# Gated DeltaNet block on one core: the first value convolution of the second half of heads, made behind the query convolutions instead of behind the decay exponentials

## The chip, the core and the metric

The kernel runs on one core of a Trainium2 chip. The core has five engines with queues of their own: TensorE (PE, matrix products; PEld is its weight load), VectorE (DVE), ScalarE (ACT), GpSimd (POOL) and SyncE (SP, which here issues the DMA transfers). Each engine works through its queue in order; semaphores make it wait for others. The metric is the device time of one execution in microseconds (us), as a median of runs.

## The reference

One transformer layer on x of 1024 tokens by 1024 features, in float32:

```python
h = _rmsnorm(x, norm_attn_g[l]) * (1.0 + sc1) + sh1
proj = h @ w_in[l]
q_a, k_a, v_a, q_d, k_d, v_d, z_d, b_d, a_d = jnp.split(proj, split_points, axis=-1)
y_attn = _dilated_attention(q_a, k_a, v_a, rel_bias)
y_delta = _gated_deltanet(q_d, k_d, v_d, z_d, b_d, a_d, conv_w[l], a_log[l], dt_bias[l], delta_norm_g[l])
x = x + g1 * (jnp.concatenate([y_attn, y_delta], axis=-1) @ w_out[l])
h = _rmsnorm(x, norm_ffn_g[l]) * (1.0 + sc2) + sh2
x = x + g2 * ((jax.nn.silu(h @ w_gate[l]) * (h @ w_up[l])) @ w_down[l])
```

The part that matters here is the DeltaNet: 8 heads of 64 features. Its q, k and v go through a causal convolution of width 4 along the tokens and a silu, q and k are normalised to length 1, and then a recurrence over chunks of 64 tokens follows:

```python
q, k, v = jnp.split(jax.nn.silu(_causal_conv(jnp.concatenate([q, k, v], axis=-1), conv_w)), 3, axis=-1)
a_mat = jnp.where(strict, jnp.einsum('nbhcd,nbhed->nbhce', k_beta, kc) * decay, 0.0)
rhs = jnp.concatenate([vc * bc[..., None], k_beta * jnp.exp(gcum)[..., None]], axis=-1)
sol = lax.linalg.triangular_solve(a_mat + jnp.eye(CHUNK), rhs, left_side=True, lower=True, unit_diagonal=True)
qk = jnp.where(causal, jnp.einsum('nbhcd,nbhed->nbhce', qc, kc) * decay, 0.0)
```

`decay` is the exponential of differences of a running sum, `u` and `w` are the two parts of `sol`, and a scan over the chunks carries a 64x64 state per head.

## The kernel before

The kernel computes the modulation, the normed input and the projections (each as three float32r products of high and low halves), the DeltaNet, the dilated attention, the output projection and the feed-forward part, in that order as a whole. The DeltaNet is made in two halves of 4 heads, `delta(0)` and `delta(1)`; a half has two pairs of heads, and a pair fills 128 partitions. Tiles of the second half bear the numbers 2 and 3: `vd2` and `vd3` are its convolved values, `kd2`, `qd2` and so on its keys and queries.

A half consists of these steps:

- Convolutions (`conv`, L549): a scaled copy on ACT (L551), three multiply-and-add steps on DVE (L553), a silu on ACT (L557). For the second half those of k and q are made early, in `delta_early` at the end of the first half, and go through DRAM (`cv_d`); `xp_k`, `xp_q`, `xp_v` are the loaded inputs.
- `delta_turn`: transposes on PE (`trq`, `trk`), squares on ACT (`sqq`, L744) and sums on DVE (`eq`, `rk`, L748), from which the norms come.
- `delta_rows` (L701): four loads of 512 KB that spread the decay's running sums over all partitions, into `dt1_0` to `dt1_3`, one per head. They have the tag `lu` with five buffers; `vd2` and `vd3` have the same tag.
- `delta_prep` (L756): `lr`, `rk` and `nbp` on ACT and DVE, a transpose of `nbp` on PE (`ps_bp`, L781), 32 exponentials of the decay on ACT (L771, 8 for each head), the products of k with k and of q with k on PE (`kk`, L800), their multiplication by the decay on DVE (L806), stores of its blocks to DRAM (`lt_d`, L813), exponentials `eb` on ACT (L839) and the product `qd` times `eb` on POOL (L840).
- `delta_v` (L845): for each pair the convolution of the values, transposes on PE (`trv`, L857), and the product with beta on DVE (`vb`, L860).
- `delta_inverse`: loads the blocks as `nt`, inverts them in a row of small DVE steps (L886, L890), goes through DRAM as `tn`, and completes the inverse on PE (`lv`, L918).
- `delta_scan`: the recurrence.

While these steps run, PE is given the matmuls of other projections as filling: `g_z` (the gate), `g_va` (the attention's values, L613) and, in between, `mods` (the modulation, L211). `turn(name)` puts an amount of this filling, by a table `FILL` of microseconds, ahead of a named step; the table has 12.8 for `trv2_0` and 10.24 for `trv3_0`. `until(...)` runs the filling until a projection is complete. What the program text says is then put in order, on each engine, by a list scheduler that goes by the order of the text, by its cost estimates and by explicit `issue_after` relations. So a part that is written elsewhere also changes the places of its neighbours.

Of the kernel before, what the change touches and what calls it, by code (L numbers as in the profile page):

```python
# [10 lines left out]
F32 = mybir.dt.float32  # L11
# [7 lines left out]
P = 128  # L19
# [63 lines left out]
def build(tc, I, out):  # L83
# [758 lines left out]
            )  # L842
        st.update(nbp=nbp, nbg=nbg, eq=eq, kt=kt, lts=lts, qks=qks, gs=gs)

    def delta_v(g, st, vps):  # L845
        st["vb"] = []
        for q in range(2):
            hp = 2 * g + q
            vd = pd.tile([P, T], F32, name=f"vd{hp}", tag="lu", bufs=5)
            conv(8 + hp, vps[q](), vd)  # L850
            vb = pd.tile([P, 8, P], F32, name=f"vb{hp}", tag="vb", bufs=2)
            bh = beta[:, st["gs"]].rearrange("p (n h) -> p n h", n=8)[:, :, 2 * q : 2 * q + 2]
            for hf in range(2):
                ps = sbank(f"trv{hp}_{hf}")
                with turn(f"trv{hp}_{hf}"):
                    for j in range(4):
                        nc.tensor.transpose(  # L857
                            ps[:, j * P : (j + 1) * P], vd[:, (4 * hf + j) * P : (4 * hf + j + 1) * P], ident
                        )
                nc.vector.tensor_tensor(  # L860
                    out=vb[:, 4 * hf : 4 * hf + 4].rearrange("p n (e d) -> p n e d", e=2),
                    in0=ps.rearrange("p (n e d) -> p n e d", n=4, e=2),
                    in1=bc(bh[:, 4 * hf : 4 * hf + 4], 64), op=ALU.mult,
                )
            st["vb"].append(vb)
# [324 lines left out]
    def fetch(i, name):  # L1190
        xp = pr.tile([P, T], F32, name=f"xp_{name}", tag="xp", bufs=2)
        nc.sync.dma_start(xp, _.pj[i])
        return xp

    def delta_early():

        for j in range(4):
            kind, q = ("k", j) if j < 2 else ("q", j - 2)
            t = pr.tile([P, T], F32, name=f"cv{j}", tag="dt", bufs=2)
            conv((4 if kind == "k" else 0) + 2 + q, fetch(j, f"{kind}{2 + q}"), t)  # L1200
            delta_turn(1, kind, q, t, norms=norms[1])
            nc.sync.dma_start(_.cv[j], t)

    marks = {}
    norms = [delta_norms(g) for g in range(2)]

    def delta(g):
        st = {}
        kt = []
        for j in range(4):  # L1210
            kind, q = ("k", j) if j < 2 else ("q", j - 2)
            hp = 2 * g + q
            t = pd.tile([P, T], F32, name=f"{kind}d{hp}", tag=f"{kind}d", bufs=2)
            (kd if kind == "k" else qd)[hp] = t
            if g == 0:
                conv((4 if kind == "k" else 0) + hp, xps[j], t)
                kt.append(delta_turn(g, kind, q, t, norms=norms[0], keep=kind == "k"))
                if j == 1:
                    nc.scalar.activation(norms[0]["lr"], norms[0]["rk"], AF.Ln, bias=eps1)
            else:  # L1220
                nc.sync.dma_start(t, _.cv[j])
                if kind == "k":
                    kt.append(delta_turn(g, kind, q, t, keep=True))
        delta_prep(g, st, norms[g], kt[0:2], delta_rows(g))
        if g == 1:
            until(lambda: "vd" in done)
        delta_v(g, st, [lambda q=q: vxp[q] if g == 0 else fetch(4 + q, f"v{2 + q}") for q in range(2)])
        delta_inverse(g, st)
        until(lambda: ("qd", "z1")[g] in done)
        delta_scan(g, st)  # L1230
        if g == 0:
            delta_early()

    delta(0)
    delta(1)
    until(lambda: EARLY - 1 in done)
    run(mods)

# [763 lines left out]
```

## Time and profile before

| what | value |
|---|---|
| median of 3 runs (lowest, highest) | 1402.27 us (1399.55, 1403.21) |
| the profiled execution | 1399.13 us |
| its span in the profile | 1397.3 us |
| PE busy | 1343.9 us, 96% of the span |
| DVE, ACT, POOL busy | 63%, 47%, 20% of the span |
| mean granted clock of PE | 0.991 |
| DMA, moved over the span | 245.68 MB |

The profile's page shows one execution. A row of a timeline has the start in us from the span's start, the length, the engine, the line of the kernel, the operation with output and inputs, the shape and the number of instructions that it stands for; in brackets stands how long the engine was idle ahead of it and what ended that. A row of waits has the waiting instruction, the one waited for, and then the time in total, how many times, and the longest. A row of a table of stretches has the stretch, its length, the busy time of each engine with the number of its instructions, then PE's granted clock (1.00 is full speed), the share in which the DMA engines were busy, and GB/s.

### The profile page before, as it was taken

What the parts mean: (1) busy time and instruction counts of PE and PEld (TensorE: products, weight loads), DVE (VectorE), ACT (ScalarE), POOL (GpSimd) and SP (SyncE); (2) the same over time, 40 slices, a digit from 0 to 9 for tenths busy, and PEclk for the clock granted to TensorE, in tenths of its full rate; (3) what the DMA queues carried; (4) which work ended last, traced back from release to release, by engine and by line L of the source; (5) the groups of instructions that cost most, each with busy time, mean ns of one, the idle gap of its engine ahead of it and who ended that gap; (6) DMA issues with size and microseconds to landing.
All of it is one profiled execution on the core that took longest, in us unless ns stands there. A gap on an engine that the chain in (4) does not pass through costs nothing.

```text
span 1397.3 us, 24428 instructions
## 1 busy us (share of the span) xinstructions
PE 1343.9 (96%) x8984; PEld 1109.9 (79%) x8984; DVE 878.8 (63%) x1677; ACT 661.4 (47%) x1287; POOL 283.6 (20%) x267
## 2 busy tenths in 40 slices
PE   8999999998999899999999999999999999999998
PEld 5778877888888777778877788888888888888876
DVE  3688484656836433676238977667575776474497
ACT  4498424356234254775157633333333333444455
POOL 2346412443213244443262000000000000000000
PEclk9999999999999999999999999999999999999999
DMA  8666575486352455541584355455453665766585
GB/s 310 230 190 168 160 212 168 131 259 184 106 152 69 124 141 177 152 110 58 187 269 151 113 159 181 158 163 173 133 200 108 213 210 191 255 222 192 195 262 197
DMA packets 169872, 245.68 MB, mean 176 GB/s; under 512 B 32566, under 2 KB 73831, under 8 KB 169752
## 3 DMA queue, kind: packets, MB, share of 16 engines
q1 hardware_dynamic: 169752, 244.12, 55.3%
q8 instruction: 71, 1.16, 0.3%
q14 instruction: 49, 0.40, 0.1%
HBM read 181.30 MB, written 67.48 MB: 178 GB/s over the span
## 4 chain that ended last, share of the span: by engine, by line
PE 53%; DVE 5%; DMA 3%; issue 2%; ACT 2%; POOL 1%; SPq 0%; DVEq 0%; ACTq 0%; POOLq 0%
PE wua L1596 9%; PE wga L1596 8%; PE X L1796 6%; PE wuc L1596 4%; PE wgc L1596 4%; PE wo L590 4%; PE g_a L590 3%; PE wgb L1596 2%; PE Z L1796 2%; PE Y L1796 2%; PE wub L1596 2%; PE y L1353 2%; PE tr L1332 2%; PE S L1308 1%; PE S L1309 1%
## 5 line engine op out<-in xcount | busy, mean ns | idle before, releaser
L1586 DVE TENSOR_TENSOR wl_db<-wr_db,wh_db 128x512 fp32r<-128x512 f32 x77 | 52.9, 690 | 66.4 <-ACT wh_db L1585 66.4
L1585 ACT CAST wh_db<-wr_db 128x512 fp32r<-128x512 f32 x77 | 47.4, 620 | 85.7 <-PE X L1796 39.4
L1312 DVE CUSTOM_DVE_ANT_0 X<-S,ng 128x512 f32<-128x512 f32 (+3 forms) x64 | 36.9, 587 | 57.2 <-PE S L1309 43.7
L1319 POOL TENSOR_SCALAR X<-X,sc 128x128 f32<-128x128 f32 (+7 forms) x64 | 48.7, 764 | 76.3 <-DVE sc L1318 72.3
L1796 PE MATMUL X<-wl_db,wh_da 128*128 128x512 f32 x160 | 62.4, 390 | 0.3 <-DVE wl_db L1586 0.3
L1796 PE MATMUL X<-wh_db,wl_da 128*128 128x512 f32 x160 | 62.3, 389 | 0.0
L1796 PE MATMUL X<-wh_db,wh_da 128*128 128x512 f32 x160 | 62.3, 389 | 0.0
L1317 ACT ACTIVATE X<-X,sc 128x128 f32<-128x128 f32 (+7 forms) x64 | 49.5, 775 | 24.3 <-DVE sc L1312 22.7
L1586 DVE TENSOR_TENSOR wl_da<-wr_da,wh_da 128x512 fp32r<-128x512 f32 x77 | 52.8, 685 | 3.7 <-ACT wh_da L1585 3.6
L1585 ACT CAST wh_da<-wr_da 128x512 fp32r<-128x512 f32 x77 | 47.5, 616 | 15.0 <-DMA wr_da<-ao_d 8.1
L590 PE MATMUL g_a<-hh,wh_a 128*128 128x512 f32 x128 | 52.7, 412 | 0.0
L590 PE MATMUL wo<-yl,wh_wo 128*128 128x512 f32 x128 | 50.6, 396 | 1.9 <-DVE yl L1416 1.9
L590 PE MATMUL g_a<-hh,wl_a 128*128 128x512 f32 x128 | 51.7, 404 | 0.0
L590 PE MATMUL wo<-yh,wh_wo 128*128 128x512 f32 x128 | 51.6, 406 | 0.0
L590 PE MATMUL g_a<-hl,wh_a 128*128 128x512 f32 x128 | 51.4, 401 | 0.0
L590 PE MATMUL wo<-yh,wl_wo 128*128 128x512 f32 x128 | 51.1, 399 | 0.0
L1332 PE MATMUL tr<-ident,X 128*128 128x128 f32 x288 | 45.8, 278 | 5.1 <-POOL X L1319 2.4
L1585 ACT CAST wh_wg_s<-wg_s 128x512 fp32r<-128x512 f32 x33 | 20.5, 623 | 57.6 <-PE wuc L1596 24.4
L1332 PEld LDWEIGHTS tr<-ident,X 128*128 128x128 f32 x288 | 32.8, 140 | 17.0 <-POOL X L1319 6.2
L231 POOL TENSOR_TENSOR wl_wo<-wr_wo,wh_wo 128x512 fp32r<-128x512 f32 x24 | 32.2, 1344 | 59.1 <-ACT wh_wo L230 54.9
L1585 ACT CAST wh_wu_s<-wu_s 128x512 fp32r<-128x512 f32 x33 | 20.4, 621 | 43.8 <-PE wga L1596 17.2
L1585 ACT CAST wh_wg<-wr_wg 128x512 fp32r<-128x512 f32 x31 | 19.2, 622 | 46.3 <-PE wua L1596 18.9
(553 smaller groups left out, 4370.0 us busy)
## 6 DMA issues: line engine op xcount, KB each, us to landing
wm<-in_wada SPq DMA_DIRECT2D x44, 512.0 KB, 6.3
wr_da<-ao_d SPq DMA_DIRECT2D x77, 256.0 KB, 3.1
wr_wu<-in_wu SPq DMA_DIRECT2D x50, 256.0 KB, 2.7
wr_wg<-in_wg SPq DMA_DIRECT2D x48, 256.0 KB, 2.9
ao_d<-a SPq DMA_DIRECT2D x44, 256.0 KB, 2.4
wr_wd<-in_wdn SPq DMA_DIRECT2D x44, 256.0 KB, 3.0
wr_db<-wt_d SPq DMA_DIRECT2D x44, 256.0 KB, 2.7
ao_d<-as SPq DMA_DIRECT2D x33, 256.0 KB, 2.0
```

The source lines that it names most:

```text
L231: (eng or nc.gpsimd).tensor_tensor(out=lo[:, :n], in0=raw[:, :n], in1=hi[:, :n].bitcast(F32), op=ALU.subtract)
L590: last[0] = nc.tensor.matmul(ps, a[:, w0], b[k0 + k4][:, cs], start=(i == 0), stop=(i == n - 1))
L1308: nc.tensor.matmul(ps[:, 0 : c1 - c0], QS[:, qs], KS[:, c0:c1], start=True, stop=False)
L1312: nc.vector.tensor_tensor_reduce(out=X[:, c0:c1], in0=ps[:, 0 : c1 - c0], in1=ng[:, u + c0 : u + c1], scale=1.0, scalar=(3e38 if m is None ...
L1317: nc.scalar.activation(X[:, 0:nk], X[:, 0:nk], AF.Exp, scale=-1.0, bias=m, accum_out=sc[:, 2:3])
L1319: nc.gpsimd.tensor_scalar(out=X[:, 0:nk], in0=X[:, 0:nk], scalar1=sc[:, 3:4], scalar2=0.0, op0=ALU.mult, op1=ALU.add)
L1332: nc.tensor.transpose(ps[:, (kb - c0) * P : (kb - c0 + 1) * P], X[:, kb * P : kb * P + P], ident)
L1353: ins = nc.tensor.matmul(yps[64 * e : 64 * e + 64, (q % 4) * P : (q % 4 + 1) * P], va[:, kb, 64 * e : 64 * e + 64], ets[q % 2][e][:, kb, : ...
L1585: nc.scalar.copy(hi, src)
L1586: (eng or nc.vector).tensor_tensor(out=lo, in0=src, in1=hi.bitcast(F32), op=ALU.subtract)
L1596: nc.tensor.matmul(ps, a[:, w0], b, start=(first and k == 0 and n_ == 0), stop=(k == 3 and n_ == 2), skip_group_check=True,)
L1796: nc.tensor.matmul(bank[b], a[:, ts_], w, start=(first and n_ == 0), stop=(last and n_ == 2), skip_group_check=True,)
```

## The change

In the second half the convolution of `vd2` is written at the end of `delta_early`, right behind the convolutions of the queries; before, it was written in `delta_v`, behind all of `delta_prep`. Because `vd2` and the four `dt1` tiles share the buffers of `lu`, the four loads of `delta_rows(1)` are written ahead of it, and so is the `until` that completes the projection of the values. `delta_v` then takes the tile made early. The convolution of `vd3` stays where it was.

```diff
-    def delta_v(g, st, vps):
+    def delta_v(g, st, vps, early):
         st["vb"] = []
         for q in range(2):
             hp = 2 * g + q
-            vd = pd.tile([P, T], F32, name=f"vd{hp}", tag="lu", bufs=5)
-            conv(8 + hp, vps[q](), vd)
+            if hp == 2:
+                vd = early
+            else:
+                vd = pd.tile([P, T], F32, name=f"vd{hp}", tag="lu", bufs=5)
+                conv(8 + hp, vps[q](), vd)
...
             nc.sync.dma_start(_.cv[j], t)
+        rows = delta_rows(1)
+        until(lambda: "vd" in done)
+        vd = pd.tile([P, T], F32, name="vd2", tag="lu", bufs=5)
+        conv(10, fetch(4, "v2"), vd)
+        return rows, vd
...
-    def delta(g):
+    def delta(g, made=(None, None)):
...
-        delta_prep(g, st, norms[g], kt[0:2], delta_rows(g))
+        delta_prep(g, st, norms[g], kt[0:2], made[0] or delta_rows(g))
         if g == 1:
             until(lambda: "vd" in done)
-        delta_v(g, st, [lambda q=q: vxp[q] if g == 0 else fetch(4 + q, f"v{2 + q}") for q in range(2)])
+        delta_v(g, st, [lambda q=q: vxp[q] if g == 0 else fetch(4 + q, f"v{2 + q}") for q in range(2)], made[1])
...
-        if g == 0:
-            delta_early()
-
-    delta(0)
-    delta(1)
+        return None if g else delta_early()
+
+    delta(1, delta(0))
```

How it moves the instructions is seen on ACT, from the last decay exponentials to the value convolutions' silus. Before (`va0` are evictions of the filling):

```order
L771 ACTIVATE dt1_3_3559<-dt1_3_3559,lr1_1383 128x128 x8
L839 ACTIVATE eb2_3825<-eb2_3825 128x1024
L839 ACTIVATE eb3_3831<-eb3_3831 128x1024
L551 ACTIVATE vd2_3836<-xp_v2_3837,cw_1056 128x1024
L1088 COPY va0_0_4108<-g_va0_0_4083 128x256
L1088 COPY va0_1_4137<-g_va0_1_4112 128x256
L557 ACT_TABLE_LOAD
L557 ACTIVATE vd2_3836<-vd2_3836 128x1024
L551 ACTIVATE vd3_4045<-xp_v3_4046,cw_1056 128x1024
```

On ACT after the change, from the last square of the query norms to the first decay exponential (the eb exponentials are now followed by the copy of vd3):

```order
L744 ACTIVATE sqq2_1_3435<-trq2_1False_3430 128x512
L551 ACTIVATE vd2_3530<-xp_v2_3531,cw_1056 128x1024
...
L767 ACT_TABLE_LOAD
L767 ACTIVATE rk1_1378<-lr1_1383 128x32
...
L230 CAST wh_va0_3_4078<-wr_va0_3_4077 128x512
L557 ACT_TABLE_LOAD
L557 ACTIVATE vd2_3530<-vd2_3530 128x1024
...
L771 ACT_TABLE_LOAD
L771 ACTIVATE dt1_0_3510<-dt1_0_3510,lr1_1383 128x128
```

The copy and the silu of vd2 have moved from behind all 32 decay exponentials to ahead of the first. On DVE the same stretch, from the last step of the query convolutions to `ps_bp`'s copy, was before:

```order
L553 SCALAR_TENSOR_TENSOR cv3_3439<-xp_q3_3440,cw_1056,cv3_3439 128x1021
L766 TENSOR_SCALAR lr1_1383<-lr1_1383 128x32
L748 TENSOR_REDUCE eq1_1379<-sqq2_1_3435 128x4x2
L768 TENSOR_TENSOR lr1_1383<-lr1_1383,Gc_1330 128x32
L775 SCALAR_TENSOR_TENSOR nbp1_1380<-beta_1329,rk1_1378 128x32
```

and is on DVE after the change:

```order
L748 TENSOR_REDUCE eq1_1379<-sqq2_1_3435 128x4x2
L553 SCALAR_TENSOR_TENSOR vd2_3530<-xp_v2_3531,cw_1056,vd2_3530 128x1023
L748 TENSOR_REDUCE eq1_1379<-sqq3_0_3498 128x4x2
L553 SCALAR_TENSOR_TENSOR vd2_3530<-xp_v2_3531,cw_1056,vd2_3530 128x1022
L553 SCALAR_TENSOR_TENSOR vd2_3530<-xp_v2_3531,cw_1056,vd2_3530 128x1021
L218 STREAM_TRANSPOSE t12_1334<-tri_69 128x128
L748 TENSOR_REDUCE eq1_1379<-sqq3_1_3506 128x4x2
L222 TENSOR_TENSOR mod_131<-t12_1334,bada_127 128x4
L768 TENSOR_TENSOR lr1_1383<-lr1_1383,Gc_1330 128x32
L772 TENSOR_SCALAR eq1_1379<-eq1_1379 128x32
L775 SCALAR_TENSOR_TENSOR nbp1_1380<-beta_1329,rk1_1378 128x32
```

The three steps of vd2 now stand ahead of the small operations on `lr` and `nbp`. On PE the transposes of vd2 stood before behind 42 and 7 matmuls of `g_va0`, counted from the last kk product, with the `mods` in between:

```order
L613 MATMUL g_va0_2_4141<-wl_va0_2_4073,hh5_99 128x256
L613 MATMUL g_va0_2_4141<-wh_va0_3_4078,hh6_100 128x256
L857 MATMUL trv2_0_3845<-ident_64,vd2_3836 128x128 x4
L857 MATMUL trv2_1_4039<-ident_64,vd2_3836 128x128 x4
L613 MATMUL g_va0_2_4141<-wh_va0_3_4078,hl6_108 128x256
L613 MATMUL g_va0_2_4141<-wl_va0_3_4079,hh6_100 128x256
```

On PE after the change they follow the last kk product:

```order
L800 MATMUL kk1_2_1_k_3812<-kd3_3553 128x128
L800 MATMUL kk1_3_1_k_3813<-kd3_3553 128x128
L860 MATMUL trv2_0_3845<-ident_64,vd2_3530 128x128 x4
L860 MATMUL trv2_1_4039<-ident_64,vd2_3530 128x128 x4
L613 MATMUL g_va0_1_4112<-wh_va0_1_4066,hh3_97 128x256
L613 MATMUL g_va0_1_4112<-wh_va0_1_4066,hl3_105 128x256
```

Fifteen of the `g_va0` matmuls that stood behind the kk products now stand between them. The transposes of vd3 stand, after the change, 63 matmuls of `g_va0` and the `mods` behind those of vd2, and 23 matmuls of `g_va0` further ahead than before; from there to the end PE's order is the same.

## The prediction

> **What bounds the kernel now.** I read the page first, then the waits of TensorE (PE), then each engine in order of time around the place of the change, last the granted clock there. The page:
>
> ```profile
> PE 1343.9 (96%) x8984; PEld 1109.9 (79%) x8984; DVE 878.8 (63%) x1677; ACT 661.4 (47%) x1287; POOL 283.6 (20%) x267
> PE 53%; DVE 5%; DMA 3%; issue 2%; ACT 2%; POOL 1%; SPq 0%; DVEq 0%; ACTq 0%; POOLq 0%
> ```
>
> PE is busy for 1343.9 of 1397.3 us, and the chain that ended last is mostly PE. So a change is worth what it takes from PE's idle time and from the time in which PE's clock is low. The longest waits of PE, in the whole kernel and (the last two) between 280 and 440 us:
>
> ```profile
> PE trv L857 <- ACT vd L557: 5.7, 2, 3.8
> ...
> PE yt L1065 <- DVE o L1055: 1.8, 3, 1.2
> PE g_va L613 <- ACT va L1088: 1.5, 1, 1.5
> ```
>
> The largest is the transposes of the values (trv) waiting for the silu that ends their convolution: 5.7 us in two waits, of which the 3.8 us one is that of vd2, the first pair of the second half. In PE's order of time (start, length, what, wait ahead of it):
>
> ```profile
> 325.86 1.99 PE L800 MATMUL kk_q<-qd,kd 64*128 64x128 f32 x28
> 327.59 0.37 PE L800 MATMUL kk_k<-kd 64*128 64x128 f32 x1
> ...
> 330.63 0.39 PE L613 MATMUL g_va<-wh_va,hh 128*128 128x256 f32 x1
> 335.86 1.08 PE L211 MATMUL mods<-wm,cc 128*32 128x128 f32 x32
> 341.73 1.97 PE L857 MATMUL trv<-ident,vd 128*128 128x128 f32 x8 [3.76 <-ACT vd L557]
> 343.35 0.56 PE L613 MATMUL g_va<-wh_va,hl 128*128 128x256 f32 x1
> 347.12 0.37 PE L613 MATMUL g_va<-wh_va,hh 128*128 128x256 f32 x1
> 347.32 0.29 PE L613 MATMUL g_va<-wh_va,hl 128*128 128x256 f32 x1
> 351.28 0.29 PE L613 MATMUL g_va<-wh_va,hl 128*128 128x256 f32 x1
> 351.41 1.03 PE L857 MATMUL trv<-ident,vd 128*128 128x128 f32 x8
> 352.20 0.36 PE L613 MATMUL g_va<-wl_va,hh 128*128 128x256 f32 x1
> ```
>
> PE stands for 3.76 us. Then eight transposes take 1.97 us where the next eight, for vd3, take 1.03. From 343.35 to 347.12, both counted, 18 g_va matmuls start, 0.22 us apart; 34 from 347.32 to 351.28 start 0.12 apart. The clock says why (last three columns: granted clock, DMA share, GB/s):
>
> ```profile
> 340.00:345.00 5.00, 3.27 (x16) 3.27 (x17) 1.42 (x3) 2.88 (x4) 0.00 (x0) 0.55 0.98 296
> 345.00:350.00 5.00, 5.00 (x35) 5.00 (x35) 3.81 (x3) 1.24 (x3) 0.00 (x0) 0.77 0.48 141
> ```
>
> It is 0.55, then 0.77. At full clock the transposes would occupy 0.79 us (351.41 to 352.20) and 18 g_va matmuls 2.16, together 2.95 us; they took 5.59 (341.73 to 347.32). So the low clock behind the gap cost 2.6 us.
>
> Why vd2 is late stands on ScalarE (ACT), VectorE (DVE) and GpSimd (POOL):
>
> ```profile
> 307.76 0.59 ACT L744 ACTIVATE sqq<-trq_1False 128x512 f32<-128x512 f32 x1
> 319.80 8.88 ACT L771 ACTIVATE dt<-dt,lr 128x128 f32<-128x128 f32 x30
> 330.03 1.06 ACT L839 ACTIVATE eb<-eb 128x1024 f32<-128x1024 f32 x1 [0.40 <-issue]
> 330.99 1.13 ACT L551 ACTIVATE vd<-xp_v,cw 128x1024 f32<-128x1024 f32 x1
> 339.33 1.28 ACT L557 ACT_TABLE_LOAD   x1 [4.38 <-DVE vd L553]
> 340.62 1.06 ACT L557 ACTIVATE vd<-vd 128x1024 f32<-128x1024 f32 x1
> ...
> 332.16 3.38 DVE L553 SCALAR_TENSOR_TENSOR vd<-xp_v,cw,vd 128x1023 f32<-128x1023 f32 x1 [1.48 <-ACT vd L551]
> 344.96 3.92 DVE L553 SCALAR_TENSOR_TENSOR vd<-xp_v,cw,vd 128x1023 f32<-128x1023 f32 x3 [0.54 <-ACT vd L551]
> ...
> 329.71 4.75 POOL L840 TENSOR_TENSOR qd<-qd,eb 128x1024 f32<-128x1024 f32 x2 [6.30 <-DMA lt_d<-dt]
> ...
> 302.04 0.34 SPq L1192 DMA_DIRECT2D xp_v<-pj_d  x1
> ```
>
> The copy that begins vd2's convolution stands behind the 32 decay exponentials (they end at 319.80 + 8.88 = 328.68) and the two eb exponentials. Its first DVE step takes 3.38 us where vd3's three take 3.92 together, about 1.3 each: it began as POOL's second qd product did, and ended 1.08 us after it (329.71 + 4.75 = 334.46). So vd2 is complete only at 341.68, though its input was asked for at 302.04.
>
> **The change part by part.** *Amount of work.* No arithmetic, transfer or table load is added or removed: vd2's copy (1.13), three DVE steps (1.3 each) and silu (1.06) are the same, earlier in their queues, and ACT changes its table four times in this stretch as before. Zero.
>
> *vd2 leaves the place behind the exponentials.* The 3.76 us gap and the 2.6 us of low clock go, together 6.4, if nothing takes their place.
>
> *vd2 now stands in front of the exponentials.* Its copy can start on ACT at about 308.4, behind the square at 307.76, and its silu at about 316. Copy and silu put 2.2 us in front of the exponentials; I replayed the new order with the old durations, and the last decay exponential ends at about 330.7 instead of 328.7. The input allows that start: it has 6.3 us from its issue. Other loads of this size took
>
> ```profile
> dt<-G_d SPq DMA_DIRECT2D x3, 512.0 KB, 7.4
> kd<-cv_d SPq DMA_DIRECT2D x2, 512.0 KB, 4.1
> ```
>
> so between 2 us early and 1 us late; I take no wait, and 1 us is in the range.
>
> *Who waits for the exponentials.* DVE multiplies each kk product by a decay, and PE's next kk product waits for the bank that this frees; so PE runs the kk products at ACT's pace. Unhindered it starts 28 of them in 1.73 us (325.86 to 327.59), 0.062 each. The 112 of 319.55 to 330.63 with the six g_va matmuls among them need 112 x 0.062 + 6 x 0.12 = 7.6 of those 11.1 us, so PE has 3.5 us of hidden waiting there. In the new order 15 g_va matmuls (1.8 us) move up between the kk products and fill the time for which the exponentials are late. The kk products then end at about 332.4 and vd2's transposes right behind them at 333.4. In the old order the same work, kk, 15 g_va and eight transposes, makes 330.63 + 1.8 + 1.0 = 333.4. So the later exponentials cost nothing up to 2 us; past that, the cover is gone and each microsecond costs one.
>
> *DVE.* vd2's three steps now stand ahead of lr and nbp, and the transpose ps_bp on PE waits for nbp.
>
> ```profile
> 310.03 0.18 DVE L775 SCALAR_TENSOR_TENSOR nbp<-beta,rk 128x32 f32<-128x32 f32 x1
> 312.36 3.75 POOL L231 TENSOR_TENSOR wl_va<-wr_va,wh_va 128x512 fp32r<-128x512 f32 x3
> ```
>
> nbp moves from 310.0 to about 316: the steps are 3.9 us, and POOL's wl_va products (1.25 each) hold one or two of them as the qd product did above. PE reaches ps_bp at about 315.6 and waits 0.7 to 1.9 us. This lies ahead of the kk products and inside the 3.5 us which they would wait anyway: zero, if no low clock follows.
>
> *POOL* makes its qd products 2 us later, behind the eb exponentials. They can no longer hold vd2's steps, but can hold vd3's. *SP* issues the same loads; the second kd load now stands behind two dt loads and still some 20 us ahead of its use: zero. The load of nt moves two rows back: zero, by the slack below.
>
> *What is late next: vd3.* Its tile takes vd2's buffer, so its copy waits for vd2's transposes, 333.4. Copy 1.15, DVE steps 3.92, table load 1.28, silu 1.06 make 7.4 us, so 340.8 undisturbed. I add 1.9 for vd2's products with beta, which stand ahead on DVE, and for POOL's second qd product, which runs to 336.6: the silu ends at 342.7. Between the transposes PE has 63 g_va matmuls (7.6) and the mods (1.08) and arrives at 333.4 + 8.7 = 342.1. That is a new wait of 0.6 us. Bounds: none (undisturbed), and 0.8 (the full 2.1 us above 1.3 of the row at 332.16 added to 340.8).
>
> *Behind it.* PE is through vd3's transposes at 343.7, and after 23 g_va matmuls (2.8), which before came ahead of them, at 346.5 against 352.2: 5.7 us earlier. From there PE's order is the old one. The inverse has to keep up:
>
> ```profile
> 393.08 1.33 DVE L923 STREAM_TRANSPOSE U<-tn 32x256 f32<-32x256 f32 x3 [7.04 <-DMA tn<-tn_d]
> 405.80 0.59 PE L918 MATMUL lv<-tn,dt 32*32 32x32 f32 x25
> ```
>
> Its load of tn is there 12 us before PE uses it, and its whole chain moves some 5 us forward with vd3; it gives nothing back. Sum: -3.76 - 2.6 + 0.6 = -5.7 us. Against the profiled execution, 1399.13 us (span 1397.3), that is 1393.4. The three timed runs have a median of 1402.27, 3.1 above it; the same subtraction gives **1396.6 us**.
>
> *The clock.* Whether a short wait lowers it decides 2.6 us. Two other waits of PE and the clock behind them:
>
> ```profile
> 133.33 0.28 PE L781 MATMUL ps_bp<-ident,nbp 128*32 128x128 f32 x1 [1.19 <-DVE nbp L775]
> 135.00:140.00 5.00, 5.00 (x45) 4.88 (x43) 4.79 (x8) 5.00 (x19) 2.24 (x2) 0.66 0.60 152
> 147.57 1.09 PE L857 MATMUL trv<-ident,vd 128*128 128x128 f32 x8 [1.93 <-ACT vd L557]
> 150.00:155.00 5.00, 5.00 (x66) 4.80 (x67) 4.11 (x5) 1.55 (x4) 1.68 (x2) 1.00 0.63 194
> ```
>
> Behind 1.19 us, in the same transpose of the first half, the clock was 0.66; behind 1.93 us it was full. So a wait of 0.6 to 1.9 us may bring a low clock or not; I take none, and put one into the rivals. The Trainium skill, TensorE: Matmul & The Clock Gate, section HAM oscillation, has the rule that PE's clock falls only behind gaps of more than about 3.4 us. By that rule the 3.76 us gap has its drop, as the trace shows, and no wait of the new order would have one, so the sum would stay; the row at 133.33 speaks against it as a sharp bound.
>
> **The rivals.** *A: the gain shrinks below 0.3%* (4.2 us, about what a measurement of this kernel tells from no change). A low clock of 2.6 us follows the wait for vd3, or the wait is 2 to 3 us long because POOL holds two of its DVE steps. Gain 5.7 - 2.6 = 3.1 or 5.7 - 2.1 = 3.6, with both 1.0: 1398.7 to 1401.3. For it speaks the row at 133.33; against it, that POOL has only one qd product left when vd3's steps begin.
>
> *B: slower.* POOL holds every one of vd2's three steps for the 3.38 us of the row at 332.16. Then nbp and lr come at 309.6 + 10.1 = 319.7 instead of 316, PE stands 4.1 us at ps_bp, the clock falls (2.6), and of these 6.7 us the kk products hide 3.5. If the same holding makes vd3's wait 2.7 us and the clock falls there too (2.6), the losses are 8.5 against 6.4: 1404.4. It decides where the new waits, less 3.5, and low clocks together pass 6.4 us, which is a last exponential at about 336.4 if that alone is late. Against it: ACT makes the wh_va casts one at a time in the new order, so POOL's wl_va products have pauses in which the steps get through.
>
> *C: no effect,* 1402.3: the inverse or the scan takes it all back. Against it stand the 12 us at lv. That the convolution would not really move is excluded: in ACT's and DVE's new order it stands ahead of the exponentials.
>
> **How the numbers follow.** Forecast, with a gain of 4.2 to 7: 0.63. A: 0.16. C: 0.07. B: 0.14, all counted as slower. So faster 0.63, same 0.23, slower 0.14. The range reaches from the full 6.4 us, a further low-clock phase that happens not to occur (2.6) and 2 us for the spread of the timed runs, 1391, to the end of B, 1404; the likeliest case alone spans 1394 to 1398.5.
>
> **What would show it.** Right: waits of trv of 0 to 1 us at about 332 and 342; clock 1.00 from 330 to 350; vd2's silu at about 316, the last decay exponential ending at about 330.7; no wait at lv. Wrong: a wait for vd3's silu of over 2 us, a clock under 0.8 between 315 and 350, or exponentials that end after 333.

## The result, and the profile after

The changed kernel takes 1404.58 us (median of 20 runs, 1399.57 to 1410.10), the kernel before in the same series 1400.90 us (20 runs, 1396.11 to 1403.80). The ratio is 1.0027, 95% interval 1.0014 to 1.0040: the change costs 2 to 6 us, where 5.7 us less were forecast. The profiled execution took 1404.82 us, its span is 1403.1 us.

The engines' busy time on the page after the change:

```profile
PE 1350.7 (96%) x8984; PEld 1114.8 (79%) x8984; DVE 877.0 (63%) x1677; ACT 661.7 (47%) x1287; POOL 284.1 (20%) x267
```

TensorE (PE) is busy 6.8 us longer with the same 8984 matmuls. Part of that is a lower clock: the granted clock of this execution is 0.988 against 0.991, which is 3.6 us more lost over the span. Its waits after the change, in the whole kernel (what it waited for, total in us, times, longest):

```profile
PE g_va L613 <- ACT va L1091: 3.9, 1, 3.9
PE ps_bp L781 <- DVE nbp L775: 2.5, 2, 1.7
PE trv L860 <- ACT vd L557: 0.2, 1, 0.2
```

The 3.8 us wait of the transposes for vd2's silu is gone, and vd3's is 0.2 us. In its place stand a wait of 1.7 us at ps_bp (the other of its two waits is the first half's) and one of 3.9 us at g_va, where before there were 1.5.

Where the time went is read in two steps. First, both traces were laid beside each other matmul by matmul. The same matmul starts 3.3 us later in the profile after already at 304.6 us, ahead of the changed place, where the order of work is the same: in that trace PE's clock was low for 13.7 us between 105 and 240 us, and for 3.4 us in the trace before. That part is a difference between two executions. From 309.5 to 354.5 us the changed kernel gains 2.2 us. From 379.5 to 406.2 it loses 3.6 us. So the changed place and what hangs on it lose 1.4 us in these two traces; the rest of their 5.8 us lies elsewhere, the 3.3 us ahead of the place and 1.1 us behind 406.

Second, the queues. ScalarE (ACT) after the change, from the last query silu to the decay exponentials; start, length, what, idle time ahead and what ended it:

```profile
309.86 1.06 ACT L557 ACTIVATE cv<-cv 128x1024 f32<-128x1024 f32 x1
311.56 1.15 ACT L551 ACTIVATE vd<-xp_v,cw 128x1024 f32<-128x1024 f32 x1
319.31 1.06 ACT L557 ACTIVATE vd<-vd 128x1024 f32<-128x1024 f32 x1
323.44 0.40 ACT L771 ACTIVATE dt<-dt,lr 128x128 f32<-128x128 f32 x1
325.71 0.59 ACT L746 COPY kt<-trk_1True 128x512 f32<-128x512 f32 x1 [1.87 <-PE trk_1True L738]
326.19 1.57 ACT L771 ACTIVATE dt<-dt,lr 128x128 f32<-128x128 f32 x5
329.74 0.37 ACT L1091 COPY va<-g_va 128x256 f32<-128x256 f32 x1 [1.98 <-issue]
330.01 7.71 ACT L771 ACTIVATE dt<-dt,lr 128x128 f32<-128x128 f32 x26
```

Counted from the end of that silu (310.92), vd2's silu ends at 9.45, as forecast (9.5), and the first exponential starts at 12.5. But then ACT stands twice: 1.87 us for the transposes trk_1 of kd3, and 1.98 us in front of the eviction of g_va's first block, which in the new order stands among the exponentials. The profile names nothing that the second wait was for ("issue"), but the last of the block's 24 matmuls (the row at 329.27 below) ends 0.08 us before the eviction. The last exponential ends at 26.8, forecast 23.1, before 21.1.

PE in the same stretch says why ACT has to stand:

```profile
320.62 0.28 PE L781 MATMUL ps_bp<-ident,nbp 128*32 128x128 f32 x1 [1.66 <-DVE nbp L775]
324.69 0.97 PE L738 MATMUL trk_1True<-ident,kd 128*128 128x128 f32 x4
329.27 0.39 PE L613 MATMUL g_va<-wl_va,hh 128*128 128x256 f32 x1
339.66 1.10 PE L860 MATMUL trv<-ident,vd 128*128 128x128 f32 x8
349.68 1.09 PE L860 MATMUL trv<-ident,vd 128*128 128x128 f32 x8 [0.18 <-ACT vd L557]
```

The transposes trk_1 stand behind ps_bp, which waits for nbp behind vd2's DVE steps, and behind nine g_va matmuls, which run at low clock (PE's clock in the first of the last three columns):

```profile
318.00:322.00 4.00, 2.34 (x24) 2.02 (x23) 3.13 (x11) 3.97 (x7) 3.72 (x4) 1.00 0.93 316
322.00:325.50 3.50, 3.50 (x18) 3.12 (x16) 0.00 (x0) 1.81 (x3) 2.55 (x2) 0.51 1.01 385
```

What makes nbp late is not the number of DVE's steps alone. DVE and GpSimd (POOL) after, and the same small step eq (L772) before, while POOL stood idle:

```profile
314.55 3.49 DVE L553 SCALAR_TENSOR_TENSOR vd<-xp_v,cw,vd 128x1022 f32<-128x1022 f32 x2
319.23 1.24 DVE L772 TENSOR_SCALAR eq<-eq 128x32 f32<-128x32 f32 x1
320.39 0.18 DVE L775 SCALAR_TENSOR_TENSOR nbp<-beta,rk 128x32 f32<-128x32 f32 x1
314.59 5.84 POOL L231 TENSOR_TENSOR wl_va<-wr_va,wh_va 128x512 fp32r<-128x512 f32 x3
...
317.21 0.18 DVE L772 TENSOR_SCALAR eq<-eq 128x32 f32<-128x32 f32 x1
```

Beside POOL's wl_va products two of vd2's steps take 3.49 us instead of 2.6 (2 x 1.28), and the step eq, which in the new order stands ahead of nbp, takes 1.24 instead of 0.18. Together that is 2.0 us, more than PE's wait of 1.66.

So each engine waits for the other: POOL slows DVE's steps, these hold nbp, nbp holds PE, PE holds trk, trk holds ACT's exponentials, and these hold DVE and PE.

The second loss is on the DMA queue of SyncE (SP). After, with the last step of DVE's loop, ACT's evictions and PE's wait:

```profile
387.75 0.19 DVE L893 TENSOR_TENSOR tt<-tt,tm 128x31 f32<-128x31 f32 x1
387.97 0.32 SPq L896 DMA_DIRECT2D tn_d<-tt  x1
388.12 0.64 ACT L1100 COPY sp_a<-g_a 128x256 f32<-128x256 f32 x2
388.50 1.12 SPq L1275 DMA_DIRECT2D raw<-qk_d  x2
390.78 0.38 SPq L898 DMA_DIRECT2D tn<-tn_d  x1
391.25 2.58 SPq L229 DMA_DIRECT2D wr_a<-in_wd  x1
393.88 0.43 SPq L1101 DMA_DIRECT2D qk_d<-sp_a  x1
...
396.96 0.37 ACT L1091 COPY va<-g_va 128x256 f32<-128x256 f32 x1 [8.20 <-DMA qk_d<-sp_a]
397.39 0.58 PE L613 MATMUL g_va<-wh_va,hh 128*128 128x256 f32 x1 [3.89 <-ACT va L1091]
```

and before:

```profile
386.07 0.32 SPq L893 DMA_DIRECT2D tn_d<-tt  x1
386.48 0.38 SPq L1098 DMA_DIRECT2D qk_d<-sp_a  x1
388.74 0.37 SPq L895 DMA_DIRECT2D tn<-tn_d  x1
389.20 2.92 SPq L1098 DMA_DIRECT2D qk_d<-sp_a  x2
...
393.67 0.65 ACT L1088 COPY va<-g_va 128x256 f32<-128x256 f32 x2 [4.24 <-DMA qk_d<-sp_a]
394.09 0.39 PE L613 MATMUL g_va<-wh_va,hh 128*128 128x256 f32 x1 [1.48 <-ACT va L1088]
```

SP stands at the store of tn until the inverse's DVE loop is done, and at the load of tn until that store has landed. The four stores qk_d of a spilled projection (a0_0) stand behind it in both kernels. Until the first of them is done the four eviction buffers are taken, ACT can't evict g_va, and PE has no bank for the next block. Counted from the last query silu, PE is ready for this matmul at 82.6 instead of 85.0. It starts at 86.47 instead of 86.49. All that had been won is gone there, and behind the 3.89 us the clock falls:

```profile
390.00:400.00 10.00, 6.11 (x42) 5.90 (x41) 1.74 (x4) 0.75 (x2) 0.00 (x0) 0.86 0.95 228
```

In the table all times are counted in us from the end of the last query silu, as differences of row starts and ends in each profile; the wait is the longest single one, and "PE at g_va" is the start of the matmul at which PE waits.

| kernel | last decay exp ends | trv of vd2 | trv of vd3 | load of tn issued | wait at g_va | PE at g_va |
|---|---|---|---|---|---|---|
| before | 21.1 | 34.1 | 43.8 | 81.1 | 1.5 | 86.5 |
| before_again | 21.0 | 34.1 | 42.8 | 80.2 | 1.3 | 85.3 |
| changed kernel | 26.8 | 28.7 | 38.8 | 79.9 | 3.9 | 86.5 |
| rows_only | 22.2 | 35.2 | 42.7 | 79.9 | 1.5 | 85.3 |
| silu_late | 22.8 | 27.1 | 37.4 | 80.6 | 1.4 | 83.1 |
| small_first | 27.9 | 29.9 | 39.9 | 82.2 | 1.3 | 83.0 |
| va0_late | 24.3 | 28.0 | 37.9 | 78.0 | 1.4 | 83.3 |
| four_before | 20.6 | 33.6 | 42.2 | 79.3 | none | 83.0 |
| four_after | 25.3 | 27.2 | 37.3 | 77.7 | none | 80.9 |
| small_four | 26.7 | 28.6 | 38.6 | 80.8 | none | 80.2 |

### The profile page after: what moved, and what is told of

The parts are those of the page before. It is cut to its first block, busy times and chain, and to the rows that moved or that the text cites. A ratio compares the mean times of both kernels' runs of the same rounds, so it can differ in the third digit from the quotient of the medians.

```text
span 1403.1 us, 24422 instructions
## 1 busy us (share of the span) xinstructions
PE 1350.7 (96%) x8984; PEld 1114.8 (79%) x8984; DVE 877.0 (63%) x1677; ACT 661.7 (47%) x1287; POOL 284.1 (20%) x267
## 4 chain that ended last, share of the span: by engine, by line
PE 54%; DVE 5%; DMA 3%; issue 2%; ACT 2%; POOL 1%; SPq 0%; DVEq 0%; ACTq 0%; POOLq 0%
PE wua L1602 9%; PE wga L1602 8%; PE X L1802 6%; PE wo L590 5%; PE wgc L1602 4%; PE wuc L1602 4%; PE g_a L590 3%; PE Z L1802 3%; PE wgb L1602 2%; PE y L1359 2%; PE Y L1802 2%; PE wub L1602 2%; PE tr L1338 2%; PE S L1314 1%; PE S L1315 1%
## 5 line engine op out<-in xcount | busy, mean ns | idle before, releaser
L1591 ACT CAST wh_db<-wr_db 128x512 fp32r<-128x512 f32 x77 | 47.5, 622 | 85.3 <-PE X L1802 39.4
L613 PE MATMUL g_va<-wh_va,hh 128*128 128x256 f32 x128 | 38.6, 301 | 3.9 <-ACT va L1091 3.9
```

Of the source, the lines that this page charges most:

```text
L613: last[0] = nc.tensor.matmul(ps[:, :n], a[k][:, ts_], b[:, w0], start=(i == 0), stop=(i == 23))
L1591: nc.scalar.copy(hi, src)
```

## The experiments

The theory after the two traces: the exponentials are late through ACT's two waits, and SP's queue at tn takes what is left. Rivals: the new order of the loads on SP alone; low clock phases that come by chance; the inverse itself as the bound. The kernel before was timed along in each series: 1402.24 us (29 runs) for the first four kernels, 1404.58 (11) for the next four, 1402.86 (30) for the last four. The three series ran on three chips, so each kernel is compared with the kernel before of its own series (the ratios).

**rows_only.** Only the loads and the `until` early, vd2's convolution at its old place:

```diff
-            if hp == 2:
+            if early is not None and hp == 2:
...
         rows = delta_rows(1)
         until(lambda: "vd" in done)
-        vd = pd.tile([P, T], F32, name="vd2", tag="lu", bufs=5)
-        conv(10, fetch(4, "v2"), vd)
-        return rows, vd
+        return rows, None
```

> Only the four loads of the decay rows and the call that completes the projection of the values are made early; vd2's convolution stays behind the decay exponentials, so ACT's order is that of the kernel before and only SP's differs. My theory, that the loss comes from ACT's waits in front of and among the exponentials and is completed by the wait for the evictions of g_va at about 394 us, expects a time within 2 us of the kernel before, trv waiting 3.5 to 4 us for vd2's silu, and the last decay exponential 9 us after the first, as before. The rival, that the new order of the loads on SP makes the changed kernel slow, expects 3 us or more over before, with waits of PE or ACT for a load between 300 and 350 us.

1400.01 us (12 runs), ratio to before 0.9989 (0.9971 to 1.0008): no loss, so the order of the loads is not the cause. The trace disagrees with the expectation in one point: trv waited 0.5 us in two waits, not 3.8. There the kk products ran at low clock for 10 us:

```profile
322.00:328.00 6.00, 6.00 (x39) 5.65 (x39) 3.01 (x5) 6.00 (x22) 2.46 (x2) 0.61 0.66 185
328.00:334.00 6.00, 6.00 (x55) 6.00 (x53) 3.70 (x7) 5.91 (x14) 1.99 (x1) 0.54 0.35 71
```

PE came to trv as late as the silu did. Here a low clock ahead of a wait ate the wait and so cost less than its length.

**before_again.** The kernel before, unchanged, for a second profile.

> The kernel before once more, for a second profile. My theory expects the order of work and the late silu of vd2 to be the same, PE waiting 2 to 4 us for it, with low clock phases at other places than in the first profile. If the wait is under 1 us here, the 3.8 us of the first profile were not typical, and my forecast started from too large a gain.

The wait for vd2's silu is 3.8 us again, and the clock is low for 3.4 us behind it instead of 6.8; its one time is 1402.49 us. So the gap was typical. At half speed 3.4 us of low clock cost 1.7 us, against the 2.6 us of the sum.

**silu_late.** vd2's copy and DVE steps early, the silu behind the exponentials:

```diff
-        nc.scalar.activation(dst, dst, AF.Silu)
+        if silu:
+            nc.scalar.activation(dst, dst, AF.Silu)
...
-        conv(10, fetch(4, "v2"), vd)
+        conv(10, fetch(4, "v2"), vd, silu=False)
...
                 vd = early
+                nc.scalar.activation(vd, vd, AF.Silu)
```

> vd2's copy and its three DVE steps are made early as in the changed kernel, its silu behind the decay exponentials. So the table load and the silu leave the place in front of the exponentials, and the eviction of g_va's first block no longer stands among them. My theory expects the exponentials to run without the 2 us wait for g_va's first block and to end 2 to 4 us earlier than in the changed kernel (counted from the last query silu), no wait of more than 1.5 us at either trv, and a time 1 to 4 us below the changed kernel if the later wait at g_va does not take it all. The rival, that low clock phases which come by chance make the difference, expects the same time as the changed kernel within 1 us.

The exponentials run through, all 32 in a row, and end at 22.8, 4.0 us earlier than in the changed kernel:

```profile
324.96 9.47 ACT L772 ACTIVATE dt<-dt,lr 128x128 f32<-128x128 f32 x32
```

They start 0.8 us later than there and run 9.5 us instead of 14.3. The silu and its table load (2.34 us) left the place ahead of them too, so the 4.0 us are not the price of the waits alone. PE passes vd3's transposes 1.4 us earlier than in the changed kernel. Behind that the wait at g_va is 3.0 us in three waits. The time is 1403.74 us (12 runs; 1.0011, 0.9993 to 1.0028 to before): no gain of time could be measured, which is what the rival expected of the time. The exponentials did move as the theory has it; what they win is partly given back at g_va.

**small_first.** lr, rk, nbp and ps_bp written ahead of vd2's convolution:

```diff
+        delta_small(1, norms[1])
         rows = delta_rows(1)
```

(`delta_small` holds these lines of `delta_prep`, unchanged.)

> The changed kernel with lr, rk, nbp and ps_bp written ahead of vd2's convolution, so that vd2's DVE steps no longer stand ahead of them. My theory expects the 1.7 us wait at ps_bp and the low clock behind it to go, ACT's wait of 1.9 us for the transpose trk to go with it, and the kk products to end 2 us earlier; but one more change of ACT's table (1.3 us) falls among the exponentials. At about 394 us PE's wait for the evictions of g_va grows by what was won unless the inverse moves along. Time: 0 to 3 us below the changed kernel. The rival, that ps_bp's wait is hidden by the exponentials anyway, expects no change of the end of the kk products.

The wait at ps_bp is gone, and so is the low clock behind it:

```profile
322.00:325.50 3.50, 3.07 (x26) 2.87 (x25) 3.18 (x5) 2.01 (x4) 0.66 (x1) 1.00 1.00 368
```

ACT's wait for trk is gone with it, which shows that link of the chain; in its place stands one for a weight load (fetched by DMA):

```profile
324.85 0.62 ACT L230 CAST wh_a<-wr_a 128x512 fp32r<-128x512 f32 x1 [1.48 <-DMA wr_a<-in_wd]
```

But two more table changes (1.28 us each) stand in this order among the exponentials, which end at 27.9, and the kk products end 1.1 us later than in the changed kernel, not 2 us earlier: that part of the expectation was wrong. The time is 1402.24 us (12 runs; 0.9997, 0.9981 to 1.0013).

**act_stores, before_stores.** All stores of evicted va blocks and spilled projections issued by ACT, in the changed kernel and in the kernel before:

```diff
-            nc.sync.dma_start(_.va[c][:, :, tb].rearrange("i p d -> p i d"), ...)
+            nc.scalar.dma_start(_.va[c][:, :, tb].rearrange("i p d -> p i d"), ...)
...
-                nc.sync.dma_start(dst[:, HALF * hf + 256 * i : HALF * hf + 256 * i + 256], t)
+                nc.scalar.dma_start(dst[:, HALF * hf + 256 * i : HALF * hf + 256 * i + 256], t)
```

> The changed kernel with the stores of the evicted blocks of va and of the spilled projections issued by ACT behind each eviction and no longer by SP. In the changed kernel SP stands at the store and the load of tn until the inverse's DVE loop is done, the stores of qk and va stand behind it, their buffers stay taken, ACT's eviction waits 8 us and PE 3.9 us at g_va. My theory expects this wait to shrink below 1 us, the low clock behind it to go, and 2 to 5 us below the changed kernel in time. The rival, that PE's wait comes from the transfers' own time and not from the queue, expects a wait of over 2.5 us as before and no gain.

> The kernel before with the stores of the evicted va blocks and spilled projections issued by ACT instead of SP, vd2's convolution at its old place. My theory, that SP's queue makes PE wait at g_va at about 394 us in every kernel and cancels what is won ahead of it, expects the 1.5 us wait there to go, the 3.8 us gap at vd2's transposes to stay where the exponentials are not late, and a time 1 to 4 us above the changed kernel with the same stores, because there the early convolution is no longer given back. The rival, that the early convolution is worth nothing even without that wait, expects the two to agree within 1 us.

act_stores takes 1390.67 us (6 runs; 0.9924, 0.9903 to 0.9944), before_stores 1393.57 us (6 runs; 0.9927, 0.9903 to 0.9951). PE no longer waits at g_va in either. The gain is larger than that wait, and the most of it has nothing to do with the change, since the kernel before has it too; where the rest of it comes from is open. The 3.8 us gap did not stay in before_stores, as had been expected; its trace shows 1.0 us, with the exponentials ending at 22.2. Each against the kernel before of its own series, the two agree (0.9924 and 0.9927): that is the outcome of the rival, by which the early convolution is worth nothing even without the wait. This edit moves too much to isolate the wait; the next pair does that.

**four_after, four_before.** Only the four stores of a0_0, which stand on SP behind the load of tn, issued by ACT; the orders of PE, DVE and POOL are those of the changed kernel and of the kernel before:

```diff
-                nc.sync.dma_start(dst[:, HALF * hf + 256 * i : HALF * hf + 256 * i + 256], t)
+                (nc.scalar if name == "a0_0" else nc.sync).dma_start(dst[:, HALF * hf + 256 * i : HALF * hf + 256 * i + 256], t)
```

> The changed kernel with four stores alone moved from SP to ACT: those of the spilled projection a0_0, which stand on SP behind the load of tn. PE, DVE and POOL have the changed kernel's order. My theory, that these stores keep the eviction buffers and with them PE's g_va until SP has got past tn, expects PE's wait of 3.9 us there to fall below 0.5 us, the low clock behind it to go, the stretch from 380 to 405 us to be 5 us shorter, and the time 3 to 6 us below the changed kernel; against the kernel before 0 to 3 us faster. The rival, that PE waits for the inverse itself or for the transfers, expects the wait to stay above 2 us.

> The same four stores moved in the kernel before; PE, DVE and POOL have its order. My theory expects the 1.3 to 1.5 us wait at g_va to go, and 1 to 2 us in time, so that the early convolution is then worth what it wins in the stage from 309 to 355 us less its low clock: the changed kernel with the four stores 0 to 3 us below this one. The rival, that the early convolution is worth nothing in any case, expects the two equal.

Four stores moved in the changed kernel: 1393.13 us (7 runs), 0.9941 (0.9915 to 0.9968) of the kernel before. In the kernel before: 1399.67 us (12 runs), 0.9978 (0.9957 to 0.9999). The wait of 3.9 us is gone, and PE is busy throughout at full clock where it stood in the changed kernel (the matmul starts at 389.1 here):

```profile
380.00:390.00 10.00, 10.00 (x72) 9.42 (x71) 2.71 (x8) 2.54 (x6) 2.61 (x2) 1.00 0.73 183
390.00:400.00 10.00, 10.00 (x85) 10.00 (x85) 1.74 (x4) 2.71 (x8) 0.00 (x0) 1.00 1.00 267
```

So the wait came from the place of these stores, not from the transfers or the inverse, and with it gone the changed kernel is faster than the kernel before. Against four_before the early convolution is then worth 2.1 us at the g_va matmul (80.9 against 83.0) in the two traces, and 6.5 us in the medians, with intervals that overlap; how little of that is established is said below, with the clock.

The same place explains two rows of the table. In silu_late one and in small_first two of these four stores had come ahead of the load of tn in SP's order, so that their early matmul (83.1 and 83.0) is not owed to ACT alone.

**va0_late.** The changed kernel, with the eviction of g_va's first block held behind the last exponential:

```diff
-                nc.scalar.activation(lts[h][:, n], lts[h][:, n], AF.Exp, bias=lr[:, n, h : h + 1])
+                marks[f"exp{g}"] = nc.scalar.activation(lts[h][:, n], lts[h][:, n], AF.Exp, bias=lr[:, n, h : h + 1])
...
+            behind = tc.issue_after(marks["exp1"].ins) if c == 0 and tb == 0 and "exp1" in marks else ExitStack()
-            with urgent():
+            with urgent(), behind:
                 taken[0] = nc.scalar.copy(t, ps[:, 0:256])
```

> The changed kernel with the eviction of g_va's first block held behind the last decay exponential; the engines' other orders change by two rows of PE. My theory, that the exponentials are late because ACT stands for PE at this eviction (2 us) and at the copy of trk (1.9 us), expects the first of the two waits to go and the exponentials to end 1.5 to 2.5 us earlier after the last query silu, the kk products as much earlier, and no gain in time, since the wait at g_va near 394 us grows by as much. The rival, that the exponentials wait for data, expects the end of the exponentials to stay.

One of ACT's two waits is left, the other is gone, and the exponentials end at 24.3, 2.5 us earlier:

```profile
324.97 0.59 ACT L746 COPY kt<-trk_1True 128x512 f32<-128x512 f32 x1 [1.71 <-PE trk_1True L738]
325.45 9.17 ACT L771 ACTIVATE dt<-dt,lr 128x128 f32<-128x128 f32 x31
```

The kk products end only 0.8 us earlier, not as much as the exponentials. And the time falls, against the expectation: 1399.61 us (12 runs), 0.9969 (0.9949 to 0.9990) of the kernel before, where the changed kernel had 1.0027 (1.0014 to 1.0040). The wait at g_va did not grow, it is 1.4 us. Two things differ from the changed kernel there: the load of tn is issued at 78.0 instead of 79.9, and two qk_d stores follow it at once, as before, with no weight load between:

```profile
388.37 0.37 SPq L898 DMA_DIRECT2D tn<-tn_d  x1
388.83 2.90 SPq L1102 DMA_DIRECT2D qk_d<-sp_a  x2
393.67 0.39 PE L613 MATMUL g_va<-wh_va,hh 128*128 128x256 f32 x1 [1.42 <-ACT va L1092]
```

From the issue of tn's load to PE's start it is 5.3 us here and in the kernel before, 6.6 in the changed kernel. The 2.58 us of the weight load there are hardly its own: a store in the same place, right behind tn's load, held SP for 2.4 us in the kernel before, and another weight load 3.29 us in small_first. It seems to matter only which row stands there. One eviction that the scheduler put among the exponentials cost both: the late inverse and the worse order on SP.

**silu_stores, small_stores, small_four.** The two variants with all stores on ACT, and small_first with the four stores:

> vd2's copy and DVE steps early, its silu behind the exponentials, and the stores issued by ACT. My theory expects the stage from the last query norm to vd3's transposes to be 3 to 4 us shorter than in the kernel before, no wait of more than 1 us at g_va near 394 us, and a time 1 to 3 us below the changed kernel with ACT's stores. The rival, that low clocks fill whatever is won, expects the same time as that kernel, with a lower granted clock.

> The changed kernel with the small operations on lr and nbp ahead of vd2's convolution and the stores issued by ACT. My theory, that the wait at ps_bp brings the low clock at 322 us in most executions, expects no wait at ps_bp, no low clock between 318 and 330, 1 to 2 us less of clock loss over the runs than in the changed kernel with ACT's stores alone, and a time equal to it within 2 us, since a further table change stands among the exponentials. The rival, that the low clock there comes by chance, expects the same clock loss.

> The small operations on lr and nbp ahead of vd2's convolution, and the four stores moved to ACT. My theory expects no wait at ps_bp and so no low clock between 318 and 330, no wait of more than 0.5 us at g_va near 394, and 2 to 5 us below the kernel before. The rival, that the wins of both kinds are filled elsewhere, expects the kernel before's time within 1 us.

1393.40 us (6 runs; 0.9916, 0.9888 to 0.9944), 1390.66 us (5 runs; 0.9906, 0.9882 to 0.9931) and 1397.57 us (12 runs; 0.9968, 0.9945 to 0.9991). silu_stores did not come out clearly below act_stores (0.9916 and 0.9924 of their series' kernel before), and still waits 1.1 us at g_va; the rival's other half, a lower clock, isn't there either (0.994 in its profile, 0.990 in act_stores'). small_stores and small_four show no wait at ps_bp and no low clock between 318 and 330. Clock loss is the span times one minus the granted clock: over the runs 7.0 us in small_stores and 9.3 in act_stores, with errors of 2.0 and 1.1, so the expected difference has the right sign and isn't established. small_four starts the g_va matmul earliest of all (80.2), yet its median isn't the lowest.

**The clock over all runs.** The changed kernel's 20 runs lose 14.3 us to low clock (standard error 0.8). For the kernel before in that series no clocks are on record; its 70 runs of the three later series lose 12.4 (11.6, 13.6 and 12.6). What is left of the span at full clock is 1388.7 us (0.6) and 1388.4 (0.4). So in full-clock work no effect of the change is seen, as little as in the table's last column (86.5 against 86.5 and 85.3), and about 1.9 us (error 0.9) more goes to low clock. This compares different series: the kernel before had a median of 1400.90 us beside the changed kernel and 1402.24 to 1404.58 later. How the 3.7 us measured side by side divide into clock and work is therefore not shown.

By the same count four_after is left with 1384.4 us of full-clock work (0.8), four_before with 1384.8 (0.8), the kernel before of their series with 1388.6 (0.6). So moving the four stores is worth some 4 us in either kernel, and the early convolution is not seen in that figure either. What lies between the two is mostly low clock, 8.8 us (error 1.9, 7 runs) against 13.4 (0.6): the 3.8 us gap is gone in four_after, and the wait at ps_bp brought no low clock in its trace. That the early convolution is a gain once the stores are out of the way is likely by this pair, not established, and the pair with all stores on ACT doesn't show it.

## Why the prediction was wrong

- **The amount of work, the gap and the new start of vd2: right.** vd2's silu ended at 9.45 (forecast 9.5), ps_bp waited 1.7 us (0.7 to 1.9), vd3's transposes waited 0.2 us (0.6), and no trv waited longer. The gap of 3.76 us was typical (3.8 in the second profile). The low clock behind it was one or two phases, so 2.6 us was the upper of two values.
- **"The last decay exponential ends at about 330.7 instead of 328.7": wrong, and the first half of the loss.** It ended 3.7 us later than that. The replay let ACT run as if its inputs were there. Two rows of its new order, the copy behind trk_1 and the eviction of g_va, take their input from PE, and PE was itself late. va0_late, which takes away one of the two waits and gets 2.5 us back, shows it, and in silu_late all 32 exponentials run in a row. This leaves 5.7 - 3.7 = 2.0 of the forecast gain; 2.2 us was measured.
- **"Its load of tn is there 12 us before PE uses it ... it gives nothing back": wrong, and the second half.** The slack at lv was true and beside the point. The inverse is waited for at a second place, by SP, which stands at tn with the a0_0 stores behind it. The same section said of the changed places on SP only that the loads are the same. The row that showed the place was quoted at the start: g_va waiting 1.5 us for ACT's eviction. I never followed back what ACT waited for. four_after shows that without those four stores behind tn the wait is gone.
- **"Its whole chain moves some 5 us forward with vd3": wrong.** The chain starts with nt, which needs the stores of the decayed blocks, and these wait for the exponentials: the load of nt was issued at 40.6 where before it was at 38.2. The load of tn came 1.3 us earlier, PE 2.4 us.
- **The clock.** I took no low clock from the wait at ps_bp (0.7 to 1.9 us forecast) and left one to the rivals. The wait was to cost nothing inside the kk products' hidden waiting; it did cost, by way of trk and the exponentials and by a low clock of 3.4 us. The low clock came in the profiles of the changed kernel, silu_late, act_stores and va0_late; in four_after and silu_stores the clock stayed full behind such a wait (1.3 to 1.7 us in all six). By the rule of the Trainium skill, TensorE: Matmul & The Clock Gate, section HAM oscillation, that only gaps above about 3.4 us lower the clock, none would have come; the four traces disagree.
- **The rivals.** B had the place and the mechanism of the first loss, DVE's steps slowed by POOL ahead of nbp and PE standing at ps_bp, but not the size: the slowing came to 2.0 us, not 3.38 us for each of three steps, and fell in part on eq, which B did not name. Its 1404.4 us beside the measured 1404.58 is luck: the wait at ps_bp was 1.7 and not 4.1 us, the one for vd3 0.2 and not 2.7, and the kernel before was 1.4 us faster in this series than in the three runs it started from. C, the inverse takes it all back, was right in kind; it was set against the 12 us at lv, and it came by SP's queue instead. Together they had 0.21.

## What to carry to other kernels

When a step is moved, go through each in-order queue row by row and ask of every row in the new order where its input comes from, the engine that is to be relieved included: an eviction or a copy that takes its input from a late engine holds everything behind it. A slack is a slack only if nothing else waits for the same event: before calling a chain hidden, list what stands behind its stores and loads on the DMA queue. A wait of PE that is already in the profile, however short, can mark the place that takes back what is won ahead of it, as the 1.5 us at g_va did here. A step that is moved also gets new neighbours on other engines: look at what POOL does beside DVE's steps at the new place.

## What was not expected of the hardware

PE's clock falls on a grid. In the clock records of all 14 traces each low phase starts a multiple of 3.413 us from every other of the same trace and lasts 3.41, 6.83 or 10.24 us, at half speed (one at the very end, when PE has nothing more to do, is cut off). I added up PE's idle time within each stretch of this grid from the matmul records (all of a trace but its first 27 and last 30 us, stretches that were low themselves left out) and counted how many were followed by a low one:

```
PE idle in a stretch of 3.41 us    stretches    low clock next
under 0.6 us                            5001                 0
0.6 to 1.2                               249                 8
1.2 to 1.5                                48                 7
1.5 to 1.7                                30                13
1.7 to 1.9                                18                11
over 1.9                                  33                32
```

So here some 1.9 us of idle time within one stretch, a little over half of it, was enough in 32 of 33 cases, and between 1.5 and 1.7 us a low phase followed in nearly every second case. The same wait can cost a phase or not according to where the grid cuts it. The wait of 1.66 to 1.67 us at ps_bp lay within one stretch in the changed kernel, va0_late and (all but 0.04 us) act_stores, and a low phase followed; in four_after the grid cut it into 0.86 and 0.81 us, and none did. Of the two waits in the prediction's rows, the 1.93 us one was cut so that 1.66 us fell into one stretch, without a low phase. The 1.19 us one left 1.07 us in a stretch and had one; it is among the eight exceptions under 1.2 us. So the grid doesn't explain all, and in the range from 1.2 to 1.9 us these traces don't tell one case from the other: silu_late and silu_stores both had 1.33 us at ps_bp within one stretch, the first with a low phase, the second without. The trace can't show what is counted; six of the eight cases under 1.2 us stand at 132 to 137 us, among the first half's kk products, which use 64 of 128 rows, so idle time may not be all of it. Over the runs of equal kernels the loss to low clock ranges from 4 to 20 us, and longer runs go with more of it (correlation 0.45 to 0.7 in the four groups of runs with clocks on record): so it is a good part, not the whole, of why equal kernels differ by several microseconds.
